# Other start addresses for the weight slots and the feature tiles of a two-layer hybrid decoder trunk

## The chip, the cores and the metric

One core of a Trainium2 chip runs the whole program in one launch. The metric is the device time of one execution in microseconds, as a median of several. A profiled execution gives a trace beside it, with the start and duration of each instruction on each engine.

## The reference, cut to what matters

Two layers, each of four blocks with a residual add: a SwiGLU of width 2816, a mixer (an HGRN2 group and a forgetting-attention group behind one input projection), cross attention over 256 memory tokens, and another SwiGLU. The activations are 256 tokens by 1024 features, all in float32.

```python
for l in range(DEPTH):                                   # DEPTH = 2
    x = x + 0.5 * swiglu(rms_norm(x, ffn1_norm[l]), ffn1_w_gate[l], ffn1_w_up[l], ffn1_w_down[l])
    x = x + hybrid_mixer(rms_norm(x, mix_norm[l]), w_in[l], ...)      # w_in: 1024 x 3592
    x = x + memory_cross_attention(rms_norm(x, cross_norm[l]), rms_norm(mem, mem_norm[l]), ...)
    x = x + 0.5 * swiglu(rms_norm(x, ffn2_norm[l]), ffn2_w_gate[l], ffn2_w_up[l], ffn2_w_down[l])
return rms_norm(x, final_norm)
```

Nearly all arithmetic is the product of 256 tokens with weight matrices, and each weight is used once.

## The kernel before, in words

**Products in three parts.** A float32 operand is split into a rounded part and a remainder, both of type float32r: `hi` is a copy (ScalarE, line 140) and `lo` is the difference (VectorE, line 141); lines 144 and 145 do the same with a gain multiplied in. The helper `mm3` (lines 432 to 434) issues three matmuls for one product: high by high, then high by low, and low by high. A matmul keeps a block of 128 x 128 in the array (the stationary operand, loaded by an LDWEIGHTS) and streams the other operand past it (the moving one).

**Weights.** A list `plan` holds all pieces of weights in the order of their use. `fetch` brings a piece from HBM into one of three `raw` buffers, on the SP queue, two pieces ahead. `split` makes the two parts in slots of `SLOT` columns: seven slots named `whi` and seven named `wlo` (`N_W = 7`), used in turn. A row of 512-column pieces puts two blocks of 128 input features into one slot, the 1024-column pieces of the down and output projections one block, the 256-column pieces four, and the 260-column pieces (there are eight, for the value part of the forgetting attention) as many as fit: `n = max(1, SLOT // cw)`.

**Two ways round.** In `wstat` the weights are stationary and the features move, 256 tokens in a matmul: for each of the column blocks of a pair of pieces it goes through eight blocks of input features, three matmuls for each. As a slot holds two of those blocks, six matmuls in a row use one pair of slots, 24 make a pass over four pairs, and a pair of 512-column pieces takes four passes, 96 matmuls. In `xstat`, `xstat_first` and `rows_to_residual` the features are stationary and a row of 512 weights moves. There one block of a down projection takes 12 matmuls from one slot pair (two halves of the tokens, two halves of the columns, three parts), except in the last six blocks, which are gone through once for each half of tokens and of columns, three matmuls a visit.

**Features.** They stand as `hi` and `lo` tiles of 1024 columns (4096 bytes a partition) in the pool `sp`, whose 19 buffers hold most other work tiles too.

**Addresses.** The pools lie one behind the other in SBUF: constants (`cp`), `rawp`, `wp` with the weight slots, `sp`, `np`, `sm`. A slot of 1040 columns takes 4160 bytes, which is 64 more than a multiple of 256, so that the slots begin at four different values modulo 256: the seven `whi` at 192, 0, 64, 128, 192, 0 and 64, the seven `wlo` at 128, 192, 0, 64, 128, 192 and 0. They come up in a fixed round of seven pairs, given here as (`whi`, `wlo`) modulo 256: (192, 128), (64, 0), (0, 192), (192, 128), (128, 64), (64, 192), (0, 0). Every tile of `sp` is 4096 bytes long and begins at 64, as do the tiles of 2048 bytes in `sm`. The three `raw` buffers begin at 64, 192 and 64, the identity matrix for transposes at 128. A column block of 128 is 512 bytes, so that a slice of columns begins at the same value as its row; only the rows of the 260-column pieces (1040 bytes) begin 16 bytes further each.

**Order.** Generators for the main chain and for side tasks are driven by a clock of estimated latencies (`drive`), which writes out the order of instructions at build time; the latencies don't depend on `SLOT`.

Of the kernel before, what the change touches and what calls it, by code (L numbers as in the profile page):

```python
# [8 lines left out]
F32 = mybir.dt.float32  # L9
# [8 lines left out]
P = 128  # L18
# [7 lines left out]
EPS = 1e-6  # L26
NEG = -1.0e30
FCH = [(c, min(512, DFF - c)) for c in range(0, DFF, 512)]
SLOT = 1040
N_S4, N_W = 19, 7  # L30
TAIL = 6
HP = 100
# [13 lines left out]
def hymba_kernel(  # L46
# [8 lines left out]
    cp = ctx.enter_context(tc.tile_pool(name="cp", bufs=1))  # L55
    rawp = ctx.enter_context(tc.tile_pool(name="rawp", bufs=3))
    wp = ctx.enter_context(tc.tile_pool(name="wp", bufs=N_W))
    sp = ctx.enter_context(tc.tile_pool(name="sp", bufs=N_S4))
# [7 lines left out]
    def nm(s):  # L66
        uid[0] += 1
        return f"{s}_{uid[0]}"
# [10 lines left out]
    def smp(name="smp"):  # L79
        return pss.tile([P, 512], F32, name=nm(name), tag="smp")  # L80

    xs = cp.tile([P, NT, D], F32, name="xs")


# [63 lines left out]
    def split_block(i, k):  # L148
# [5 lines left out]
        if k % 2 == 0:  # L154
            slot[:] = [wp.tile([P, SLOT], F32R, name=nm(n), tag=n) for n in ("whi", "wlo")]
        sl = slice(k % 2 * cw, (k % 2 + 1) * cw)
# [7 lines left out]
    def split(i):  # L164
        while len(pieces) <= min(i, len(plan) - 1):
# [3 lines left out]
            r = raws[j]  # L169
            n = max(1, SLOT // cw)  # L170
            res = []
            for k0 in range(0, nk, n):
                kk = min(n, nk - k0)
                sl = r[:, k0 * cw:(k0 + kk) * cw]
                hi = wp.tile([P, SLOT], F32R, name=nm("whi"), tag="whi")
                lo = wp.tile([P, SLOT], F32R, name=nm("wlo"), tag="wlo")
                n1 = kk if gk is None else 1
# [981 lines left out]
```

## Time and profile before

| | |
|---|---|
| median of 3 executions | 1249.28 us (1249.13 to 1250.47) |
| profiled execution, its own time | 1250.42 us |
| its span, first to last instruction | 1248.6 us |
| TensorE matmul busy | 1231.8 us, 9074 instructions |
| weight loads busy (beside the matmuls) | 1126.3 us |
| VectorE busy, ScalarE busy | 767.1 us, 641.2 us |
| mean granted TensorE clock | 0.997 |

A matmul's duration in the trace (some 0.28 us for 256 moving columns, 0.39 for 512) holds the way through the array, and neighbours overlap. What a matmul costs in a stream is the distance from its start to the next one's start, called its pitch below. In the timeline a row gives the start and the duration in us, the engine, the line, the operation, what is written and read, and the shapes.

### The profile page before, as it was taken

How to read it: one execution, taken by the hardware profiler on the slowest of the kernel's cores; microseconds unless marked ns; L12 is line 12 of the kernel's file. 1: busy time of each engine (PE TensorE's matmuls, PEld its weight loads, DVE VectorE, ACT ScalarE, POOL GpSimd, SP SyncE). 2: the span in 40 equal slices, each digit the busy share in tenths (PEclk: the TensorE clock that was granted, in tenths of full speed). 3: DMA queues.
4: the chain of work that ended last, by engine and by line, in shares of the span. 5: the costliest groups of instructions: out<-in, count | busy, mean ns of one | idle time of the engine just before them, and what ended most of it. 6: DMA issues, size and time to landing. Idle time of an engine off the chain costs nothing.

```text
span 1248.6 us, 21619 instructions
## 1 busy us (share of the span) xinstructions
PE 1231.8 (99%) x9074; PEld 1126.3 (90%) x9074; DVE 767.1 (61%) x1163; ACT 641.2 (51%) x986; POOL 38.7 (3%) x52
## 2 busy tenths in 40 slices
PE   9999999999999999999999999999999999999997
PEld 7999888989889889998889998889997898999986
DVE  7756547597775675464474464476786766545643
ACT  7555535657754454444354353366585655544532
POOL 0000000002000000000000000000020000000000
PEclk9999999999999999999999999999999999999999
DMA  9555754643453374565474555465442633555640
GB/s 319 178 180 170 239 199 157 219 158 113 169 187 134 102 253 146 192 204 201 135 253 138 200 202 202 135 220 189 147 157 102 248 117 124 177 195 169 236 169 34
DMA packets 100514, 220.76 MB, mean 177 GB/s; under 512 B 4145, under 2 KB 16705, under 8 KB 100417
## 3 DMA queue, kind: packets, MB, share of 16 engines
q1 hardware_dynamic: 100256, 219.11, 51.8%
q8 instruction: 71, 1.16, 0.4%
q10 hardware_dynamic: 160, 0.27, 0.1%
q14 instruction: 27, 0.21, 0.1%
HBM read 218.32 MB, written 1.05 MB: 176 GB/s over the span
## 4 chain that ended last, share of the span: by engine, by line
PE 91%; ACT 5%; DVE 3%; issue 1%; POOL 1%; DMA 0%; POOLq 0%; SPq 0%; ACTq 0%; DVEq 0%
PE acc L432 28%; PE acc L433 28%; PE acc L434 28%; PE pt L353 1%; ACT whi L140 1%; ACT pp L856 1%; ACT fqs L872 1%; DVE wlo L141 1%; PE al L732 1%; ACT fks L874 1%; ACT fks L873 0%; POOL mrs L334 0%; PE cpo L433 0%; DVE mem L343 0%; PE cs L433 0%
## 5 line engine op out<-in xcount | busy, mean ns | idle before, releaser
L141 DVE TENSOR_TENSOR wlo<-raw,whi 128x1024 fp32r<-128x1024 f32 (+1 forms) x356 | 426.3, 1222 | 287.0 <-ACT whi L140 286.0
L140 ACT CAST whi<-raw 128x1024 fp32r<-128x1024 f32 (+1 forms) x356 | 362.8, 1048 | 303.3 <-PE acc L434 152.4
L432 PE MATMUL acc<-xfh,whi 128*128 128x256 f32 x1536 | 434.5, 283 | 0.0
L434 PE MATMUL acc<-xfh,wlo 128*128 128x256 f32 x1536 | 431.0, 281 | 1.9 <-DVE wlo L141 1.9
L433 PE MATMUL acc<-xfl,whi 128*128 128x256 f32 x1536 | 432.0, 281 | 0.0
L434 PEld LDWEIGHTS acc<-xfh,wlo 128*128 128x128 f32 x1536 | 290.2, 189 | 2.1 <-DVE wlo L141 2.1
L433 PEld LDWEIGHTS acc<-xfl,whi 128*128 128x128 f32 x1536 | 290.9, 189 | 0.4
L432 PEld LDWEIGHTS acc<-xfh,whi 128*128 128x128 f32 x1536 | 289.5, 188 | 0.9
L432 PE MATMUL acc<-whi,hth 128*128 128x512 f32 (+1 forms) x352 | 136.4, 388 | 0.0
L433 PE MATMUL acc<-wlo,hth 128*128 128x512 f32 (+1 forms) x352 | 136.3, 387 | 0.0
L434 PE MATMUL acc<-whi,htl 128*128 128x512 f32 (+1 forms) x352 | 135.8, 386 | 0.0
L432 PE MATMUL acc<-whi,xfh 128*128 128x512 f32 (+1 forms) x256 | 95.0, 371 | 0.4 <-ACT xfh L359 0.4
L433 PE MATMUL acc<-wlo,xfh 128*128 128x512 f32 (+1 forms) x256 | 94.0, 367 | 0.0
L434 PE MATMUL acc<-whi,xfl 128*128 128x512 f32 (+1 forms) x256 | 93.6, 366 | 0.1
L434 PEld LDWEIGHTS acc<-whi,htl 128*128 128x128 f32 x352 | 66.2, 188 | 14.5
L432 PEld LDWEIGHTS acc<-whi,hth 128*128 128x128 f32 x352 | 66.1, 188 | 14.4
L433 PEld LDWEIGHTS acc<-wlo,hth 128*128 128x128 f32 x352 | 66.1, 188 | 14.0
L145 DVE SCALAR_TENSOR_TENSOR wlo<-raw,g,whi 128x512 fp32r<-128x512 f32 (+1 forms) x96 | 61.9, 702 | 26.0 <-PE acc L434 18.5
L144 ACT ACTIVATE whi<-raw,g 128x512 fp32r<-128x512 f32 (+1 forms) x96 | 58.2, 678 | 24.5 <-PE acc L433 16.7
L434 PEld LDWEIGHTS acc<-whi,xfl 128*128 128x128 f32 x256 | 48.1, 188 | 8.9 <-DVE xfl L360 0.4
L432 PEld LDWEIGHTS acc<-whi,xfh 128*128 128x128 f32 x256 | 48.1, 188 | 8.8 <-ACT xfh L359 0.6
L433 PEld LDWEIGHTS acc<-wlo,xfh 128*128 128x128 f32 x256 | 48.2, 188 | 8.5 <-DVE wlo L145 0.4
(255 smaller groups left out, 1424.4 us busy)
## 6 DMA issues: line engine op xcount, KB each, us to landing
raw<-in_ffn_w_down_dram SPq DMA_DIRECT2D x44, 1024.0 KB, 4.9
raw<-in_ffn_w_up_dram SPq DMA_DIRECT2D x40, 1024.0 KB, 5.1
raw<-in_ffn_w_gate_dram SPq DMA_DIRECT2D x38, 1024.0 KB, 5.2
raw<-in_w_in_dram SPq DMA_DIRECT2D x24, 1024.0 KB, 5.3
raw<-in_cross_wk_dram SPq DMA_DIRECT2D x8, 1024.0 KB, 5.0
raw<-in_w_out_dram SPq DMA_DIRECT2D x8, 1024.0 KB, 4.8
raw<-in_cross_wv_dram SPq DMA_DIRECT2D x8, 1024.0 KB, 5.3
raw<-in_cross_wq_dram SPq DMA_DIRECT2D x8, 1024.0 KB, 5.6
```

What stands on the lines that cost most here:

```text
L140: nc.scalar.copy(out=hi, in_=sl)
L141: nc.vector.tensor_tensor(out=lo, in0=sl, in1=hi.bitcast(F32), op=ALU.subtract)
L144: nc.scalar.mul(hi, sl, g)
L145: nc.vector.scalar_tensor_tensor(out=lo, in0=sl, scalar=g, in1=hi.bitcast(F32), op0=ALU.mult, op1=ALU.subtract)
L353: nc.tensor.transpose(pt[:, j * P:(j + 1) * P], hn[:, kt * P:(kt + 1) * P], ident)
L432: nc.tensor.matmul(ps, lhsT=lh, rhs=rh, start=start, stop=False)
L433: nc.tensor.matmul(ps, lhsT=lh, rhs=rl, start=False, stop=False)
L434: nc.tensor.matmul(ps, lhsT=ll, rhs=rh, start=False, stop=stop)
L732: nc.tensor.matmul(ps[s0:s0 + hb, c0:c0 + hb], lhsT=k[:, h, a:a + hb], rhs=rhs[:, h, a + step:a + step + hb], start=True, stop=True)
L856: nc.scalar.activation(dst, src, AF.Exp, bias=nmx[:, t:t + 1], scale=scale, accum_out=sms[:, t:t + 1])
L872: nc.scalar.copy(out=qs[own, :, sub, :], in_=qv.unsqueeze(1).to_broadcast([64, 2, S]))
L874: nc.scalar.copy(out=ks[oth, 0, sub, :], in_=kv)
```

## The change

The slots become 1024 columns (4096 bytes), and two tiles that nothing uses are put in: 8 columns (32 bytes) ahead of the constants, and 16 columns (64 bytes) ahead of the feature tiles.

```diff
-SLOT = 1040
+SLOT = 1024
+LOW_W, LOW_F = 8, 16
...
+    cp.tile([P, LOW_W], F32, name="low_w")
+    sp.tile([P, LOW_F], F32, name="low_f", tag="low", bufs=1)
     xs = cp.tile([P, NT, D], F32, name="xs")
```

All fourteen weight slots then begin at 224 modulo 256, and every tile of `sp` at 32; a column slice of either begins at the same value. The `raw` buffers move to 96, 224 and 96, the identity to 160, the larger tiles of `sm` to 32. In `split`, `SLOT // cw` stays 4 for 256 columns, 2 for 512 and 1 for 1024; for 260 it falls from 4 to 3, so that each of those eight pieces takes two slots of each kind in place of one, with 780 and 260 columns, and two copies and two subtractions.

## The prediction

> **What bounds the kernel now.** I read the page first (parts 1, 2 and 4), then the groups with their shapes kept apart, then the timeline of TensorE in two stretches.
>
> ```profile
> span 1248.6 us, 21619 instructions
> ...
> PE 1231.8 (99%) x9074; PEld 1126.3 (90%) x9074; DVE 767.1 (61%) x1163; ACT 641.2 (51%) x986; POOL 38.7 (3%) x52
> ...
> PE 91%; ACT 5%; DVE 3%; issue 1%; POOL 1%; DMA 0%; POOLq 0%; SPq 0%; ACTq 0%; DVEq 0%
> PE acc L432 28%; PE acc L433 28%; PE acc L434 28%; PE pt L353 1%; ACT whi L140 1%; ACT pp L856 1%; ACT fqs L872 1%; DVE wlo L141 1%; PE al L732 1%; ACT fks L874 1%; ACT fks L873 0%; POOL mrs L334 0%; PE cpo L433 0%; DVE mem L343 0%; PE cs L433 0%
> ...
> L434 PE MATMUL acc<-xfh,wlo 128*128 128x256 f32 x1536 | 431.0, 281 | 1.9 <-DVE wlo L141 1.9
> ```
>
> TensorE is busy for 99% of the span, and the chain that ended last is 91% TensorE, nearly all of it the three lines of `mm3`. The row of line 434 says that in 1536 matmuls of that kind the engine stood idle 1.9 us in all for a late weight slot. So nothing that feeds TensorE sets the time; what counts is how closely its matmuls follow each other, the pitch. The change touches exactly what could set that: the addresses that TensorE reads.
>
> The next two fences are the timeline of TensorE. The first is one pair of pieces in `wstat` (weights stationary, 256 columns moving), from a longer run of such pairs; only the first matmul of each slot pair is kept, so that six matmuls lie between neighbouring rows, and the outermost rows span five whole pairs of pieces, 480 matmuls.
>
> ```profile
> 485.21 0.28 PE L432 MATMUL acc<-xfh,whi 128*128 128x256 f32 x1
> ...
> 507.83 0.28 PE L432 MATMUL acc<-xfh,whi 128*128 128x256 f32 x1
> ...
> 508.54 0.28 PE L432 MATMUL acc<-xfh,whi 128*128 128x256 f32 x1
> ...
> 509.25 0.28 PE L432 MATMUL acc<-xfh,whi 128*128 128x256 f32 x1
> ...
> 509.96 0.27 PE L432 MATMUL acc<-xfh,whi 128*128 128x256 f32 x1
> ...
> 510.65 0.28 PE L432 MATMUL acc<-xfh,whi 128*128 128x256 f32 x1
> ...
> 511.36 0.28 PE L432 MATMUL acc<-xfh,whi 128*128 128x256 f32 x1
> ...
> 512.08 0.28 PE L432 MATMUL acc<-xfh,whi 128*128 128x256 f32 x1
> ...
> 512.79 0.27 PE L432 MATMUL acc<-xfh,whi 128*128 128x256 f32 x1
> ...
> 513.48 0.28 PE L432 MATMUL acc<-xfh,whi 128*128 128x256 f32 x1
> ...
> 514.19 0.28 PE L432 MATMUL acc<-xfh,whi 128*128 128x256 f32 x1
> ...
> 514.91 0.28 PE L432 MATMUL acc<-xfh,whi 128*128 128x256 f32 x1
> ...
> 515.61 0.27 PE L432 MATMUL acc<-xfh,whi 128*128 128x256 f32 x1
> ...
> 516.31 0.28 PE L432 MATMUL acc<-xfh,whi 128*128 128x256 f32 x1
> ...
> 517.01 0.28 PE L432 MATMUL acc<-xfh,whi 128*128 128x256 f32 x1
> ...
> 517.74 0.28 PE L432 MATMUL acc<-xfh,whi 128*128 128x256 f32 x1
> ...
> 518.44 0.27 PE L432 MATMUL acc<-xfh,whi 128*128 128x256 f32 x1
> ...
> 519.13 0.28 PE L432 MATMUL acc<-xfh,whi 128*128 128x256 f32 x1
> ...
> 541.75 0.28 PE L432 MATMUL acc<-xfh,whi 128*128 128x256 f32 x1
> ```
>
> From 485.21 to 541.75 are 56.54 us for 480 matmuls: a pitch of 117.8 ns. In the four passes from 507.83 on, the slot pairs come as (128, 64), (64, 192), (0, 0), (192, 128), each with six matmuls a pass. Their four stretches add up to 2.83, 2.88, 2.82 and 2.77 us for 24 matmuls each: **117.9, 120.0, 117.5 and 115.4 ns**. A row is rounded to 10 ns, so that each of these sums is good to about half a nanosecond a matmul. Shapes, engine and clock are the same; what differs is the address of the weights. The slowest pair is the one whose `whi` begins at 64, where the features begin.
>
> ```profile
> 589.50 0.40 PE L432 MATMUL acc<-whi,hth 128*128 128x512 f32 x1
> ...
> 592.29 0.39 PE L432 MATMUL acc<-whi,hth 128*128 128x512 f32 x1
> ...
> 595.10 0.39 PE L432 MATMUL acc<-whi,hth 128*128 128x512 f32 x1
> ...
> 609.00 0.40 PE L432 MATMUL acc<-whi,hth 128*128 128x512 f32 x1
> ...
> 609.70 0.39 PE L432 MATMUL acc<-whi,hth 128*128 128x512 f32 x1
> ...
> 610.39 0.39 PE L432 MATMUL acc<-whi,hth 128*128 128x512 f32 x1
> ```
>
> This is a down projection (512 weights moving). From 589.50 to 609.00 are seven slot pairs of 12 matmuls, a whole round: 19.50 us for 84, a pitch of 232.1 ns. The pair (64, 192) has 2.79 us for its 12, 232.5 ns, and (0, 0) has 2.81, 234.2 ns. In the tail, where a pair gets three matmuls, they stand the other way: 0.70 us (233) and 0.69 (230).
>
> **The change part by part.**
>
> *Weights stationary, 256 moving.* Their number is from the code: eight blocks by three for each 128 columns, 4,992 in all (the row above counts 1536 for one of the three parts of the main group, and the memory keys add 128 for each). After the change a weight row lies 192 bytes past a feature row modulo 256 (224 - 32), for both parts. In the trace that very distance belongs to weights at 0 with features at 64, the pair (0, 0): 117.5 ns, 0.3 under the mean, so a gain of 4,992 x 0.3 = 1.5 us. But there it stands right behind the pair that coincides. The other reading is that only coincidence costs: the three pairs of the quoted stretch without it have 2.83 + 2.82 + 2.77 = 8.42 us for 72, 116.9 ns, 0.9 under the mean, a gain of 4.5 us. I take the middle, **-3.0 us**. The further ends, if one state lasts throughout: every pair like the best (115.4), 2.4 x 4,992 = -12.0 us; every pair like the worst (120.0), 2.2 x 4,992 = +11.0 us.
>
> *Features stationary, 512 moving.* About 2,150 by the code (22 blocks by 4 by 3 in each of four down projections, and the first chunks, value and output projections). The pair with the distance of the changed kernel is again (0, 0), 2.1 ns over the mean in the head of that projection (+4.5 us for 2,150) and 2.1 under it in the tail (-4.5 us). I take **0**, and keep both ends.
>
> *The 260-column pieces.* Eight more copies and eight more subtractions. The extra is what an instruction costs without its columns, from two shapes of the scaled form:
>
> ```profile
> L145 DVE SCALAR_TENSOR_TENSOR wlo<-raw,g,whi 128x512 fp32r<-128x512 f32 x80 | 55.2, 746 | 23.3 <-PE acc L434 18.5 <-ACT whi L144 4.5
> L144 ACT ACTIVATE whi<-raw,g 128x512 fp32r<-128x512 f32 x80 | 51.5, 714 | 21.7 <-PE acc L433 16.3 <-DVE g L227 2.6 <-DVE sil L675 1.4
> ...
> L144 ACT ACTIVATE whi<-raw,g 128x256 fp32r<-128x256 f32 x16 | 6.8, 496 | 2.8 <-DMA raw<-in_ffn_w_up_dram 2.4 <-PE acc L433 0.4
> L145 DVE SCALAR_TENSOR_TENSOR wlo<-raw,g,whi 128x256 fp32r<-128x256 f32 x16 | 6.7, 482 | 2.7 <-ACT whi L144 2.7
> ```
>
> ScalarE: 2 x 496 - 714 = 278 ns, eight times 2.2 us. VectorE: 2 x 482 - 746 = 218 ns, eight times 1.7 us. TensorE covers it, being busy on the earlier piece, and the 1.9 us of line 434 is all that late slots cost it anywhere in that group; so 0, and up to +3.9 us if that cover is gone. The wait it could add is for a slot: these pieces now take two of the seven at a time. What queues behind a blocked copy on ScalarE is the gate activations of the mixer, and VectorE's subtraction behind it; a 512-column piece has always taken two, so I add nothing.
>
> *The clock in the mixer.* If a wait grows there, the clock may fall with it, as it does once in the second layer:
>
> ```profile
> 870.00:875.00 5.00, 3.42 (x79) 2.82 (x78) 4.97 (x7) 1.54 (x2) 0.00 (x0) 0.85 0.29 69
> 875.00:880.00 5.00, 5.00 (x94) 4.83 (x92) 3.09 (x9) 2.19 (x4) 0.00 (x0) 0.81 0.52 147
> ```
>
> The third column from the right is the granted clock: 15% of 5 us and 19% of 5 us, 1.7 us lost. A shift of the mixer can remove this or bring the like of it into the first layer: 0, between -1.7 and +1.7 us.
>
> *Everything else.* The copies and subtractions read and write the same slots at new offsets; they run ahead of TensorE, and the same cover holds. DMAs keep their number, size and order on SP, and their landing place moves by 32 bytes. In the mixer and in cross attention both operands of a matmul lie in tiles that move together, so their distance stays. Transposes pair the identity with a work tile; their distance goes from 64 (128 - 64) to 128 (160 - 32); there are a few hundred, and at 2 ns each that is under 1 us either way.
>
> *Sum.* -3.0 us against the profiled execution's own 1250.42 us gives 1247.4; that execution stood 1.1 us over the median of the runs. Against the median: **1246.3 us**.
>
> **A rule against it.** The Trainium skill, "SBUF — State Buffer", section "Who interferes with whom", gives TensorE two read ports of its own, one for the moving operand and one for the weight load, and says "PE and ACT never wait on anyone". By that the addresses would have no say, and the sum would be 0, 1249.3 us. The trace does not agree: 115.4 to 120.0 ns at one shape, by slot pair alone.
>
> **The rivals.**
>
> *A better state that lasts* (one distance everywhere, no change of slots to disturb it). For it: a stretch at 115.4 exists. Against: the trace shows 117.5 at the very distance chosen. Price: -12.0 us with the first kind alone, -16.5 with the second at 230 too; so 1233 to 1242.
>
> *Addresses have no say on the sum* (what one matmul gains the next gives back, the pitch being held by something else). For it: the five pairs of pieces from 485.21 to 541.75 have different mixes of slots, and the quoted one takes 11.30 us of a mean of 11.31. Against: the spread between slot pairs inside it. 1249.3 us.
>
> *The start at 32 costs more* (slower). Before, every moving row of 256 or 512 columns and every stationary block begins at a multiple of 64 bytes; after, all begin 32 past one. If a start off that grid costs a matmul what the coincidence costs now, it is 2.2 x 4,992 = +11.0 us and 2.1 x 2,150 = +4.5 us, 1264.8 us; at half, 1257. It decides from 0.35 ns a matmul on (2.5 us over 7,140). Against it stand the only rows that begin off the grid, the moving rows of 260, half of them 16 or 48 past it and a quarter 32 past:
>
> ```profile
> L432 PE MATMUL acc<-whi,xfh 128*128 128x260 f32 x64 | 18.4, 287 | 0.0
> ```
>
> Against line 434's 281 ns at 256 columns that is 6 ns more, of which four columns at (232.1 - 117.8) / 256 = 0.45 ns each account for 1.8. So a small extra cannot be excluded, and of stationary blocks off the grid there is no row.
>
> **How the numbers follow.** The measurement tells about 0.2%, 2.5 us, from no change. The forecast (coincidence gone, 1246.3, own range 1243 to 1250) has 0.45, of which 0.33 is faster by that bound and 0.12 within it. The lasting better state has 0.15, all faster. No say has 0.18, of which the mixer's shift puts 0.03 on the fast and 0.02 on the slow side. The start at 32 has 0.22, of which 0.01 is too small to see. So faster 0.51, same 0.26, slower 0.23. The range is 1236 to 1254: it leaves out the strongest form of the better state and the upper half of the slower rival, some 0.17 together.
>
> **What would show it.** In the timeline after, six matmuls of any slot pair should take the same 0.70 us, and 96 about 11.25 us in place of 11.31; at 0.69 the better state holds, at 0.71 nothing has changed, at 0.72 the slower rival. The down projections should keep 2.79 us for 12 matmuls. The groups of copies should show eight shapes of 780 and eight of 260 columns, and line 434's idle time should stay near 1.9 us. The prediction is wrong if the pitch moves in the 512-column stretches by over 1 ns, or if the mixers move by over 2 us through slots or clock.

## The result, and the profile after

The changed kernel takes 1256.0 us (median of 5, 1254.77 to 1256.19) against 1249.28: slower by 0.5%, ratio 1.0051, 95% interval 1.0036 to 1.0065. The forecast was 1246.3 us, a gain. The page after, in the lines that answer to those shown of before:

```profile
span 1254.4 us, 21645 instructions
...
PE 1235.3 (98%) x9074; PEld 1125.7 (90%) x9074; DVE 769.3 (61%) x1171; ACT 642.5 (51%) x994; POOL 40.1 (3%) x52
...
PE 89%; DVE 4%; ACT 2%; DMA 1%; issue 1%; POOL 1%; SPq 0%; POOLq 0%; DVEq 0%; ACTq 0%
```

The span grew by 5.8 us, TensorE's busy time by 3.5 us, and TensorE's share of the chain fell from 91% to 89%. So part of the loss is waiting. The timeline of TensorE, first matmul of three successive pairs of pieces in the same `wstat` stretch (96 matmuls between rows), and the first and last of 84 in the down projection behind it:

```profile
511.11 0.28 PE L436 MATMUL acc<-xfh,whi 128*128 128x256 f32 x1
...
522.42 0.28 PE L436 MATMUL acc<-xfh,whi 128*128 128x256 f32 x1
...
533.73 0.28 PE L436 MATMUL acc<-xfh,whi 128*128 128x256 f32 x1
...
567.64 0.40 PE L436 MATMUL acc<-whi,hth 128*128 128x512 f32 x1
...
587.25 0.39 PE L436 MATMUL acc<-whi,hth 128*128 128x512 f32 x1
```

The first three rows give 11.31 us for 96 matmuls, 117.8 ns: the mean of before, to the digit. The last two give 19.61 us for 84, 233.5 ns against 232.1. So the new addresses changed next to nothing in the one kind and cost 1.3 ns in the other. What TensorE waited for, from the list of waits, shows where the rest lies; the tiles of the first five rows belong to the mixer:

```profile
PE al L736 <- DVE kk L759: 2.4, 2, 1.2
PE fs L898 <- DVE fks L881: 1.4, 6, 0.4
...
PE pc L839 <- DVE lf L833: 1.2, 2, 0.6
PE al L736 <- DVE qf L727: 1.1, 2, 0.7
PE fs L898 <- DVE fqs L879: 1.1, 4, 0.3
...
PE acc L438 <- DVE wlo L145: 0.2, 1, 0.2
```

The three numbers are us in all, times, and the longest. In the same list before, `al` waited for `kk` 0.8 us, `fs` for `fks` 0.6, and the other three of the first five weren't among the rows shown. Each is a matmul that waits for VectorE. The last row is the wait for a late weight slot in the main products: 1.9 us before, 0.2 after. So the loss doesn't show at the matmuls that read the weights, but at the mixer's own.

VectorE's timeline in the first layer's mixer shows why. Before, and after:

```profile
295.02 1.37 DVE L141 TENSOR_TENSOR wlo<-raw,whi 128x1024 fp32r<-128x1024 f32 x1
296.32 1.27 DVE L360 TENSOR_TENSOR oTl<-hot,oTh 128x512 fp32r<-128x512 f32 x2
297.62 0.36 DVE L879 TENSOR_SCALAR fqs<-L,oh 64x256 fp32r<-64x256 f32 x1
```

```profile
296.26 4.05 DVE L145 TENSOR_TENSOR wlo<-raw,whi 128x1024 fp32r<-128x1024 f32 x3
300.23 1.27 DVE L364 TENSOR_TENSOR oTl<-hot,oTh 128x512 fp32r<-128x512 f32 x2
301.54 0.42 DVE L879 TENSOR_TENSOR fqs<-fq,fqs 64x256 fp32r<-64x256 f32 x1
```

The line numbers of these tiles are four higher after, so that the third row after is line 875 of before. In these rows VectorE takes one instruction after the other. Before, one weight subtraction stood directly ahead of `oTl` (the remainder of the HGRN2 output) and of the attention operands `fqs`; after, three do, and `oTl` begins 3.9 us later. The copies on ScalarE that such subtractions follow show where the three come from. Before, and after:

```profile
269.88 2.03 ACT L140 CAST whi<-raw 128x1040 fp32r<-128x1040 f32 x2
275.35 1.05 ACT L140 CAST whi<-raw 128x1024 fp32r<-128x1024 f32 x1 [1.30 <-DMA raw<-in_cross_wk_dram]
```

```profile
273.11 0.84 ACT L144 CAST whi<-raw 128x780 fp32r<-128x780 f32 x1
...
285.67 0.41 ACT L144 CAST whi<-raw 128x260 fp32r<-128x260 f32 x1 [1.62 <-PE acc L437]
```

Before, the last two 260-column pieces were copied by 271.9 us, and the next piece's first slot followed at 275.35. After, the copy of the last 260-column block, which needs a slot of its own, begins only at 285.67 us. It stands behind other copies of the mixer, and ScalarE idles 1.62 us for it until a TensorE matmul ends, that is, until a slot comes free. The copies of the next pieces come behind it, and their subtractions run later and closer together, three of them right ahead of `oTl`. So the order on ScalarE and VectorE is no longer that of before, although the latencies by which `drive` orders the work don't depend on the slot size.

The score matmuls `fs` then wait, and the granted clock (third column from the right) falls. The stretches 300 to 315 and 915 to 930 us before, then after:

```profile
300.00:315.00 15.00, 14.62 (x128) 14.19 (x127) 12.71 (x44) 13.84 (x33) 1.74 (x2) 1.00 0.13 37
915.00:930.00 15.00, 15.00 (x133) 14.79 (x133) 12.79 (x46) 13.79 (x34) 1.75 (x2) 1.00 0.14 47
```

```profile
300.00:315.00 15.00, 13.92 (x100) 13.32 (x100) 13.89 (x48) 12.41 (x31) 1.44 (x3) 0.89 0.32 122
915.00:930.00 15.00, 13.93 (x100) 13.31 (x99) 14.56 (x42) 13.05 (x31) 4.48 (x5) 0.89 0.39 141
```

In 15 us TensorE does 100 matmuls where it did 128 and 133. The changed kernel is late there, so that the windows don't hold quite the same work; 0.11 of 15 us is 1.7 us of clock in each layer. That the waits bring the clock down is read from their coming together; no run separates the two. The clock is not the whole loss: the execution with the highest mean granted clock, 0.998, still took 1254.77 us.

### The profile page after: what moved, and what is told of

Its sections match the earlier page's. It is cut to its first block, busy times and chain, and to the rows that moved or that the text cites. A ratio compares the mean times of both kernels' runs of the same rounds, so it can differ in the third digit from the quotient of the medians.

```text
span 1254.4 us, 21645 instructions
## 1 busy us (share of the span) xinstructions
PE 1235.3 (98%) x9074; PEld 1125.7 (90%) x9074; DVE 769.3 (61%) x1171; ACT 642.5 (51%) x994; POOL 40.1 (3%) x52
## 4 chain that ended last, share of the span: by engine, by line
PE 89%; DVE 4%; ACT 2%; DMA 1%; issue 1%; POOL 1%; SPq 0%; POOLq 0%; DVEq 0%; ACTq 0%
PE acc L436 28%; PE acc L438 27%; PE acc L437 27%; DVE wlo L145 2%; PE pt L357 1%; DMA mem<-in_mem_dram 1%; PE al L736 1%; PE warm L224 0%; ACT pp L860 0%; ACT fqs L876 0%; POOL mrs L338 0%; DVE fks L881 0%; PE cpo L437 0%; POOL hrs L805 0%; ACT whi L144 0%
## 5 line engine op out<-in xcount | busy, mean ns | idle before, releaser
L145 DVE TENSOR_TENSOR wlo<-raw,whi 128x1024 fp32r<-128x1024 f32 x364 | 428.7, 1201 | 289.9 <-ACT whi L144 289.0
L144 ACT CAST whi<-raw 128x1024 fp32r<-128x1024 f32 x364 | 364.3, 1028 | 305.0 <-PE acc L438 150.4
```

Of the source, the lines that this page charges most:

```text
L144: nc.scalar.copy(out=hi, in_=sl)
L145: nc.vector.tensor_tensor(out=lo, in0=sl, in1=hi.bitcast(F32), op=ALU.subtract)
```

## The experiments

The theory was that the loss sits in the mixers and comes from the 260-column pieces, which now take two slots of each kind; the rivals were that the addresses cause it, or both evenly. Seven kernels take the change apart.

**The cutting alone.** The slots stay at 1040 columns, and slots and features keep their addresses (as the cut pieces take more slots, later pieces come to lie on other pairs of the round):

```diff
-            n = max(1, SLOT // cw)
+            n = max(1, 1024 // cw)
```

> Only the cutting of the eight 260-column pieces is taken from the change (three blocks in one slot and one in the next), slots and features stay where they were. Theory A (the extra slots, copies and subtractions change the order of work in the two mixers, and the loss sits there): about +4 to +5 us against before, 1253 to 1255, with the loss between the input projection and the memory keys. Rival B (the new addresses are slow, in the mixers too): no change, 1249.3. Rival C (both share it evenly): about +3 us.

1254.43 us, ratio 1.0034 (1.0021 to 1.0046). The mixer's waits and the clock are those of the changed kernel:

```profile
300.00:315.00 15.00, 13.93 (x100) 13.34 (x100) 13.88 (x48) 12.39 (x31) 1.44 (x3) 0.89 0.31 124
915.00:930.00 15.00, 13.93 (x100) 13.32 (x100) 14.56 (x46) 12.62 (x32) 3.71 (x5) 0.89 0.39 140
```

**The addresses alone.** 1088 columns are 17 times 256 bytes, so slots still begin at one value, and four blocks of 260 fit:

```diff
-SLOT = 1040
+SLOT = 1088
+LOW_W, LOW_F = 8, 16
...
+    cp.tile([P, LOW_W], F32, name="low_w")
+    sp.tile([P, LOW_F], F32, name="low_f", tag="low", bufs=1)
```

> Only the addresses of the change: slots of 1088 columns (17 times 256 bytes), with the two pads, so that all weight rows begin at 224 and all feature rows at 32 as in the changed kernel, while four 260-column blocks still fit a slot; the order of instructions on every engine is that of before. Theory A: +1 to +2 us (the 512-column stretches, 233 ns a matmul for 232; the 256-column ones within 0.3 ns), 1250 to 1251.5. Rival B: 1255 to 1256, as the changed kernel. Rival C: about 1252.5.

1250.61 us, ratio 1.0008 (0.9999 to 1.0016). Theory A holds, B and C fall: the cutting accounts for 4 to 5 us, the addresses for some 1 us (the interval reaches from nothing to 2 us), and the two add up to a ratio of 1.0042 of the 1.0051.

**The same distance on the 64-byte grid** (`LOW_W, LOW_F = 16, 16`: weights at 0, features at 64).

> As the run with the addresses alone, but with pads of 64 and 64 bytes: weights at 0 and features at 64, the same distance of 192 on the grid of 64 bytes. If only the distance modulo 256 counts: the same time and pitches as with 224 and 32 (117.6 and 233 ns). If the start at 32 past the grid costs something: faster than it, by up to 2 us in the 512-column stretches.

1250.7 us, ratio 1.001 (1.0001 to 1.0019), and pitches as with 224 and 32 (117.8 and 233.3 ns). The start at 32 past the grid, my slower rival, shows no price: with the same distance the two kernels agree within 0.1 us.

**Coincidence** (no pads: weights and features at 192).

> As the run with the addresses alone, but with no pads: weights and features both begin at 192. If coincidence is what costs (120.0 ns in the slot pair at 64, where features lie at 64 too): 256-column pitch 119.5 to 120, some +8 to +10 us, 1257 to 1260. If the dear stretches came from changing slots: within 2 us of the run with 224 and 32.

1249.16 us, ratio 0.9998 (0.9989 to 1.0007). The pitch of the first kind came as expected. The total did not; it lies where the other reading put it, but by two effects that cancel:

```profile
507.57 0.28 PE L433 MATMUL acc<-xfh,whi 128*128 128x256 f32 x1
...
519.09 0.28 PE L433 MATMUL acc<-xfh,whi 128*128 128x256 f32 x1
...
565.17 0.40 PE L433 MATMUL acc<-whi,hth 128*128 128x512 f32 x1
...
584.24 0.39 PE L433 MATMUL acc<-whi,hth 128*128 128x512 f32 x1
```

96 matmuls in 11.52 us are 120.0 ns, the dear value of the pair (64, 192). But 84 of the other kind in 19.07 us are 227.0 ns, 5 ns *under* before. 2.2 x 4,992 = +11.0 us and -5.1 x 2,150 = -11.0 us cancel. No pair of before had shown this: of the pairs whose `whi` coincides with the features, each had its `wlo` elsewhere, and (64, 192) stood at 232.5.

**Instructions or slots?** The cut pieces with two copies and two subtractions, but in one slot:

```diff
+                if cw == 260:
+                    n1 = 3
                 for k in range(0, kk, n1):
-                    w = slice(k * cw, (k + n1) * cw)
+                    w = slice(k * cw, min(k + n1, kk) * cw)
```

> Before, with each 260-column piece still in one slot of each kind but written by two copies and two subtractions (780 and 260 columns): the instructions of the change without its extra slots. Theory A1 (the extra slots hold up the copies that follow, because only seven stand in the ring): no change, within 1 us of 1249.2. Rival A2 (the eight extra instructions on ScalarE and VectorE, and the order that they make, cost it): about +5 us, 1254.

1249.16 us, ratio 1.0001 (0.9992 to 1.001): the eight extra instructions on each engine cost nothing that the interval shows, as the prediction had it. The loss is the slots'. (No run gave the ring an eighth slot, which would show the same from the other side.)

**Which pair of pieces?** `n = 3` only for the first 260-column pair of each layer, then only for the second.

> Before, with only the first pair of 260-column pieces of each layer (the half used ahead of the query projection) cut into two slots; the second pair stays whole. In the cut kernel the first layer was 1.3 us late at the end of the HGRN2 level matmuls and 3.3 us late at the output projection. If the first pair causes it all: 1253 to 1254.5. If the later loss comes from the second pair: 1250.5 to 1251.5.

1251.1 us, ratio 1.0013 (1.0004 to 1.0021).

> Before, with only the second pair of 260-column pieces of each layer (the half used ahead of the memory keys) cut into two slots. The first pair alone cost 1.9 us and both together 5.2 us. If the pairs add up: 1252.5. If it takes both (a ring that is full twice, or a clock that falls only once the waits are long enough): 1249.5 to 1251.

1251.83 us, ratio 1.0018 (1.0009 to 1.0027). Apart they cost 0.13% and 0.18%, together 0.34%; within the intervals that is a sum, and 1251.83 lies between the two expectations. The clock in 300 to 315 and 915 to 930 us stays at 1.00 with the first pair cut, and falls in one layer only with the second:

```profile
300.00:315.00 15.00, 15.00 (x129) 14.74 (x129) 12.81 (x47) 13.70 (x34) 1.67 (x2) 1.00 0.15 55
915.00:930.00 15.00, 15.00 (x129) 14.78 (x127) 12.80 (x47) 13.70 (x34) 1.67 (x2) 1.00 0.16 65
```

```profile
300.00:315.00 15.00, 13.93 (x101) 13.30 (x100) 13.88 (x49) 12.47 (x31) 0.87 (x2) 0.89 0.25 90
915.00:930.00 15.00, 13.89 (x110) 12.91 (x110) 14.53 (x51) 13.05 (x33) 1.23 (x3) 1.00 0.30 119
```

VectorE's rows ahead of `oTl`, with the first pair cut and then with the second:

```profile
296.24 1.37 DVE L143 TENSOR_TENSOR wlo<-raw,whi 128x1024 fp32r<-128x1024 f32 x1
297.54 1.27 DVE L362 TENSOR_TENSOR oTl<-hot,oTh 128x512 fp32r<-128x512 f32 x2
```

```profile
294.92 4.05 DVE L143 TENSOR_TENSOR wlo<-raw,whi 128x1024 fp32r<-128x1024 f32 x3
298.89 1.28 DVE L362 TENSOR_TENSOR oTl<-hot,oTh 128x512 fp32r<-128x512 f32 x2
```

So the second pair makes the three subtractions ahead of `oTl` and `fqs` that were shown above. With the first pair cut one subtraction stands there, as before, and `oTl` is 1.2 us later than before (296.32): a delay of its own, from the part ahead of it.

**A version that uses the finding.** If the products with 256 moving columns want a distance and those with 512 want none, give each what it wants. Slots at 0, features at 64, and a piece gets an offset in its slot by its use: `ST` for weights that stand still, `MV` for weights that move (offsets in columns, for high and low parts). The two pads and the lines that give each piece its offset are left out here:

```diff
-SLOT = 1040
+SLOT = 1088
+LOW_W, LOW_F = 16, 16
+ST, MV = (0, 0), (16, 16)
...
-                hi = wp.tile([P, SLOT], F32R, name=nm("whi"), tag="whi")
-                lo = wp.tile([P, SLOT], F32R, name=nm("wlo"), tag="wlo")
+                hi = wp.tile([P, SLOT], F32R, name=nm("whi"), tag="whi")[:, offs[j][0]:offs[j][0] + kk * cw]
+                lo = wp.tile([P, SLOT], F32R, name=nm("wlo"), tag="wlo")[:, offs[j][1]:offs[j][1] + kk * cw]
```

> Slots of 1088 columns, pads of 64 and 64 bytes (slots at 0, features at 64), and weights that move (512 and 260 columns) are put 16 columns further into the slot, at 64, so that they coincide with the stationary features; weights that stand still keep the distance of 192. If the distance acts as in the runs before (117.7 ns for 256 moving at 192, 226.7 ns for 512 moving at 0): about -12 us, 1236 to 1239. If the gain of the one and the loss of the other belong together (the engine runs as a whole): within 2 us of 1249.

1238.83 us, ratio 0.9919 (0.9906 to 0.9933): the gain and the loss do not belong together. The timeline has 117.8 ns for the one kind and about 227 for the other.

**High and low parts apart** (`ST = (0, 48)`: high parts at 0, low parts at 192).

> As the run before it, with the low parts of the standing weights 48 columns further (at 192, the high parts at 0, features at 64), the slot pair that stood at 115.5 ns in long stretches of before (pitches of 118, 116 and 112 ns in turn). If that pattern lasts when every pair has it: 115.5 to 116 ns, -8 to -11 us more, 1227 to 1231. If it was the neighbours' doing: within 2 us of the run before it.

1232.38 us, ratio 0.9865 (0.9852 to 0.9879), the fastest of all, with the arithmetic and the order of instructions of before. Its timeline:

```profile
39.40 0.28 PE L439 MATMUL acc<-xfh,whi 128*128 128x256 f32 x1
...
50.50 0.28 PE L439 MATMUL acc<-xfh,whi 128*128 128x256 f32 x1
...
51.63 0.22 PE L309 MATMUL lbt<-ident,lbr 8*128 8x8 f32 x1
...
69.20 0.28 PE L439 MATMUL acc<-xfh,whi 128*128 128x256 f32 x1
...
80.51 0.28 PE L439 MATMUL acc<-xfh,whi 128*128 128x256 f32 x1
...
501.92 0.28 PE L439 MATMUL acc<-xfh,whi 128*128 128x256 f32 x1
...
513.02 0.28 PE L439 MATMUL acc<-xfh,whi 128*128 128x256 f32 x1
...
557.39 0.40 PE L439 MATMUL acc<-whi,hth 128*128 128x512 f32 x1
...
576.44 0.39 PE L439 MATMUL acc<-whi,hth 128*128 128x512 f32 x1
```

From 501.92 to 513.02 are 11.10 us for 96, 115.6 ns. The very first feed-forward block begins in the same way, with 11.10 us from 39.40 to 50.50. At 51.63 a small matmul of another task breaks into its row of products, and from there to the block's end 96 matmuls take 11.31 us (69.20 to 80.51), 117.8 ns, with the same slots, features and offsets. In the later feed-forward blocks no other matmul breaks into the long rows at 115.6. By an estimate, 720 matmuls at 2.2 ns are 1.6 us: hence 1232 and not under 1231. So the offsets alone don't set the pitch. Whether the interruption set off the change, and what is kept from then on, stays open.

The success is in part luck. The expectation took the pair with 0 and 192 for the one that stood at 115.5 ns in the trace of before, but there it takes 2.81 us for 24 matmuls (117.1 ns, first row at 115.94 us). The low value, 2.77 us in the prediction's rows, belongs to (192, 128) in one of its two places in the round; in the other it takes 2.84 us (118.3 ns, first row at 116.64 us).

**Three more offsets.** Low parts of the standing weights at 128, then at 224; then the fastest version with the low parts of the moving weights at 0.

> The fastest version so far with the low parts of the standing weights at 128 in place of 192 (high parts at 0, features at 64, moving weights at 64 with the features they meet). If any shift between high and low parts breaks the pattern of 117.5 ns: 115.5 to 116.5 ns, 1231 to 1234. If it is the distance of the low parts to the features that counts: here it is 64, where single stretches of before stood at 117.5, so 1237 to 1239.

> The same with the low parts at 224, a distance of 160, half way between 128 (115.7 ns) and 192 (117.7 ns) and off the grid of 64 bytes. If the pitch goes by the distance in steps of 64: that of one of its neighbours, 1232 or 1238. If steps of 32 count: a third value outside these.

> The fastest version so far with the low parts of the moving weights at 0 in place of 64, so that only the high parts coincide with the stationary features. If coincidence itself is what gives 226.7 ns: two matmuls of three keep it, some 229 ns, +4 to +5 us, 1236 to 1237. If a shift between the parts helps here as it did for the standing weights: under 226 ns, 1229 to 1231.

1241.06 (0.9929, 0.9917 to 0.9942), 1240.79 (0.9925, 0.9912 to 0.9937) and 1235.7 us (0.9887, 0.9874 to 0.9901). The first misses both expectations: at the same offsets, 96 matmuls take 10.88 us in the mixer (224.00 to 234.88 us, 113.3 ns) and 11.41 us in a feed-forward block (480.27 to 491.68 us, 118.9 ns). The second has the pitch of its neighbour at 192, 11.31 us for 96 (117.8 ns, from 480.23 us), but takes some 2 us more than that kernel's 1238.83; where they go is not shown. So I have no rule that gives a pitch from the offsets. The last is near the expected 1236, and the 512-column pitch is 229 ns as expected: partial coincidence gives part of the gain.

## Why the prediction was wrong, point by point

*TensorE's pitch bounds the kernel, and addresses move it*: right. The long stretches span 113.3 to 120.0 ns and 227 to 233.5 ns, and the last versions gain 0.7 to 1.4% with the same instructions at other addresses. The Trainium skill, "SBUF — State Buffer", "Who interferes with whom", gives TensorE two independent read ports and says that it never waits on anyone. If that is taken to mean that the places of its two operands have no say, these runs do not agree.

*Weights stationary, -3.0 us*: wrong size; the measured pitch is 117.8 ns where it was 117.8. I took the middle between the pair with the exact distance (117.5, -1.5 us) and the mean of all pairs without coincidence (116.9). The second holds the pair (192, 128) at 115.4, which takes 118.3 in its other place in the round: that low value hangs on more than the pair's own offsets, and the change abolishes the round. Only the first reading compared like with like, and even its 0.3 ns did not come. That weights and features at one offset cost 120.0 was right when both parts lie there. A `whi` at 64 is not enough: two pairs of the seven have it, and (64, 0) took 2.83 us for 24 (117.9 ns, first row at 115.23 us). So only one pair in seven paid the 120.0, and with all pairs alike the pitch is that of the old mean.

*Features stationary, 0*: too low by 1.3 ns a matmul, 2.8 us at 2,150. The sign is that of the head of that projection, the size less than the +4.5 us read from it, because 2.81 us for 12 is a rounded row: over the heads of three down projections of before the pair (0, 0) takes 2.79 to 2.81 us, and after the change the mean is 2.80. The tail, with three matmuls a visit, misled. The address-only run puts all addresses together at about +1 us; where the rest came back is not shown.

*The 260-column pieces, 0*: the step that failed. The instructions are free, as I had it; "a 512-column piece has always taken two, so I add nothing" was wrong. A piece that takes a slot more makes later copies wait, and here they share their two engines with the mixer's own work, on which matmuls wait (`al`, `fs` and `pc` above). The cover that I read from line 434 was the wrong one: its wait even fell, from 1.9 to 0.2 us. I had 3.9 us as the bound if the cover is gone, from the cost of the instructions; a wait for a slot is not bounded by that, and the loss was 4.2 to 5.2. The prediction did name a mixer that moves by over 2 us as a sign of being wrong, without a price for it.

*The clock*: the size was right (0.89 for 15 us in each layer, 1.7 us), and I kept it as a possible shift, not as a consequence of the slots. The drop at 865 to 880 us of the profiled execution before is gone after (1.00 in that window), and two others came.

*The rivals*: the slower one had the right sign by the wrong mechanism; the 32-byte start shows no price. The measured 1256.0 us lies 2 us above the range that ends at 1254.

## What to carry to other kernels

When one number sets both an address and a capacity, count what the capacity held: here pieces that took two slots in place of one cost 4 to 5 us, the addresses some 1. A stage's cover is read from the waits of that stage, not from those of the main products. To foresee an address effect, compare with stretches where every operand has the new distance, and don't average over states that the change removes. On a kernel bound by TensorE's pitch, the offsets of the stationary and the moving operand modulo 256 bytes are worth a sweep for each kind of product by itself: here they were worth 1.4%.

## What the runs showed of the hardware that had not been expected

The best offset depends on the kind of product: with both operands at one offset, 256 moving float32r features over stationary weights were slowest (120.0 ns, against 117.8 at a distance of 192) and 512 moving weights over stationary features fastest (227.0 against 233.5). Which operand moves and how many columns it has change together here, so no run tells which of the two decides. Three matmuls whose weights begin at 0 and 192 ran at 115.6 ns, faster than the same three at one offset (117.8); at 0 and 128 they ran at 113.3 in one part of the kernel and 118.9 in another, and at 0 and 224 at 117.8. In the fastest kernel the first feed-forward block ran at 115.6 up to an interruption at 51.63 us and at 117.8 from there on. So the pitch also hangs on something that the offsets modulo 256 don't catch; no run here tells what.
